# A squared-ReLU MLP on one core: the norm's factor moves from the up-projection to the sums of the down-projection, the ReLU to ScalarE, the residual to DRAM

## The chip, the core and the metric

The kernel runs on one core of a Trainium2 chip. Five engines with queues of their own work side by side: TensorE (PE, with its weight loads as PEld), VectorE (DVE), ScalarE (ACT), GpSimd (POOL) and SyncE (SP), which here only issues transfers. Each engine takes its instructions strictly in the order of its queue: one that waits holds back all behind it. The metric is the device time of one execution in microseconds (us).

## The reference

One layer of a hybrid decoder trunk, 1024 tokens of 1024 channels in fp32: a combined input projection feeds a pooling mixer and a gated linear recurrence, whose outputs go through an output projection onto the residual h; then come the squared-ReLU MLP, which the change touches, a per-layer gate and a final norm.

```
h = h + concat([y_pool, y_lru]) @ w_out
z = h * rsqrt(mean(h*h) + eps) * norm_mlp_g
h = h + square(relu(z @ w_up)) @ w_down          # 1024 -> 4096 -> 1024
z = rms_norm(h, norm_ple_g)
h = h + sigmoid(z @ w_ple_gate + b_ple_gate) * (p @ w_ple_proj)
out = rms_norm(h, norm_final_g)
```

The factor r = rsqrt(mean(h*h) + eps) is one positive number per token. So square(relu(r*u)) = r*r*square(relu(u)), and a token's r*r can be taken out of the sum over the 4096 channels of the down-projection.

## The kernel before, in words

**Layout.** Activations are kept transposed: channels on the 128 partitions, tokens along the free axis. `H[0..7]` is the residual, eight tiles of 128 x 1024; FIRST and SECOND are its two halves of 512 tokens. Every operand of a large product is split into a high and a low part, `hi` by ACT (line 185) and `lo = x - hi` by DVE (line 186), and a product takes three matmuls (hi by hi, hi by lo, lo by hi). On PE each matmul of 128x128 by 128x512 follows the last after 0.216 us.

**Stages by time.** Input projection, recurrence and pooling to 141 us; output projection with the residual add and the squares for the MLP's norm to about 224 us; up-projection to 512.33 us; down-projection to 802.5 us; the gate's products (`ps_e`, `ps_j`) to 900 us; then the last output.

**Up-projection** (`up_first`, `up_pair`, `up_double`, `up_last`). The 4096 channels are 16 pairs of tiles (`NPAIR`). A pair is a 2x2 block product by a fast scheme with seven products P1 to P7; pairs 4, 6, ... 14 go through `up_double`, which shares work with the pair before; the odd ones after them open with line 1003. A pair's result is `cc`, 128 x 2048 (quadrants c11, c12, c21, c22). `finish_up` then does `max(cc, 0) * R` on DVE over all 2048 columns (line 861, R the norm's factor), squares on ACT (line 863), some sums and differences on DVE that are the operands of the down-projection, and stores to DRAM (`act`). `copy` (line 880) and line 1003 move a PSUM result to its place on ACT; line 1003 makes the start value in bank `ps_b_u`, on which P6 of that pair accumulates.

**Norm** (`Norm.rstd`). The token sums come from a small matmul (`n_ps`, in the first half of the gate's norm `n2_ps`, in its second half `n2b_ps`); ACT takes the square root (line 482), DVE the reciprocal, and R is made by a transpose.

**Down-projection** (`down(n)`, 14 kinds: chunk c = 0 and 1, in each P1, P2, P4, P6, P7, P5, P3, each for four q). One product is 24 matmuls, 5.18 us. Before, every product is added straight into the residual `H` on DVE (line 843). In the last two kinds, P5 and P3 of chunk 1, finished tiles are squared at once for the next norm (`ple_in`, lines 440 and 443), while ACT and DVE also split the weights `wd_P_q` of the coming products and the first weights `wg_0`, `wg_1` and `proj` of the gate.

**Order.** The program is written in Python under a tile scheduler that orders each engine's queue when the program is built, by dependence and the place in the text; no order is written out by hand except for `pin`, `issue_after` and the like.

Of the kernel before, what the change touches and what calls it, by code (L numbers as in the profile page):

```python
# [63 lines left out]
def block_kernel(  # L64
# [44 lines left out]
    def pairs(tiles):  # L109
# [15 lines left out]
        ]  # L125
        for c in range(NCHUNK)
    ]
    edge = ctx.enter_context(tc.tile_pool(name="edge", bufs=1, side="right"))
    spread = edge.tile([P, 72], F32, name="edge")
    B = pairs(space("y", 12, F32R)) + pairs(space("y2", 4, F32R, "right"))  # L130
# [93 lines left out]
    def twice(x):  # L224
        return x.unsqueeze(1).broadcast_to([P, 2, x.shape[-1]])
# [203 lines left out]
    class Norm:  # L429
# [42 lines left out]
            in_order.clear()  # L472
            return [(hs, o)]

        def rstd(self, out, parts):


            for hs, o in parts:
                few = self.few(hs)
                nc.vector.tensor_copy(few, o[:, :16])  # L480
                nc.vector.tensor_tensor(few, few, o[:, 16:], ALU.add)
                nc.scalar.activation(few, few, AF.Sqrt, bias=eps, scale=1.0 / D)
                nc.vector.reciprocal(few, few)
                nc.vector.transpose(out[:, hs], few.unsqueeze(2).broadcast_to([P, 16, 32]))

# [372 lines left out]
    def finish_up(m, cc):  # L858

        c, t = divmod(m, CHUNK // 2)  # L860
        nc.vector.scalar_tensor_tensor(cc, cc, 0.0, twice(R), ALU.max, ALU.mult)
        for x in (cc[:, 1], cc[:, 0]):
            nc.scalar.activation(x, x, AF.Square)
        x11, x12, x22 = cc[:, 0, FIRST], cc[:, 0, SECOND], cc[:, 1, SECOND]
        t2 = E[1][:, FIRST]
        t4_t1 = E[0].rearrange("p (y s) -> p y s", y=2)
        x2 = cc[:, 1].rearrange("p (y s) -> p y s", y=2)
        dv(ALU.subtract, x12, x22, x12)
        dv(ALU.add, t2, x12, x11)
        dv(ALU.subtract, t4_t1, x2, twice(t2))  # L870

        def store_up():
            for g, x in enumerate((cc[:, 0].rearrange("p (y s) -> p y s", y=2), x2, t4_t1)):
                nc.sync.dma_start(ACT[c][g][t // 2][:, t % 2], x)
            nc.sync.dma_start(ACT[c][3][t // 2][:, t % 2, 0], t2)

        return store_up

    def copy(to, ps):
        nc.scalar.activation(by(to, ps), got(ps), AF.Copy)  # L880

    leave("y2")
    e1, *up_spare[:] = space("wu", 3, F32, "right")
# [133 lines left out]
    def up_double(m):  # L1017

        before = up_sums(m - 1)[3]
        cc, c11, c12, c21, c22 = up_sums(m)  # L1020
        left, right = QUARTERS
        a = bank(f"ps_a_u{m}")
        up_product(m, "P1", a)
        b = banks(f"ps_b_u{m}")[:, :HALF]
        nc.scalar.activation(b, a, AF.Copy, scale=-1.0)
        w12 = weights()
        z = bank(f"ps_z_u{m}")
        sub_product(z[:, left], w12[0], 1)
        v = banks(f"ps_v_u{m}")[:, left]
        nc.scalar.activation(v, z[:, left], AF.Copy, scale=-1.0)  # L1030
        d = bank(f"ps_d_u{m}")
        up_product(m, "P5", d)
        copy(c22, d)
        w54 = weights()
        sub_product(z[:, left], w12[1], 2, True)
        sub_product(z[:, right], w54[0], 5)
        nc.scalar.activation(by(c21[:, right], z[:, right]), got(z[:, right]), AF.Copy, scale=-1.0)
        up_product(m, "P6", b, more=True)
        copy(c12, b)
        x = bank(f"ps_x_u{m}")[:, left]  # L1040
        sub_product(x, w54[1], 4)
        copy(c21[:, left], x)
        w63 = weights()
        sub_product(v, w63[0], 6, True)
        take(before[:, right], v, before[:, right], True)
        sub_product(z[:, right], w63[1], 3, True)
        both = before.rearrange("p (b a j) -> p b a j", b=2, a=2)
        add(both, z.rearrange("p (b j a) -> p b a j", b=2, a=2))
        store = finish_up(m - 1, up_sums(m - 1)[0])
        up_product(m, "P2", a, more=True)  # L1050
        copy(c11, a)
        store()
        sub_product(v, weights()[0], 7, True)
        both = c21.rearrange("p (b a j) -> p b a j", b=2, a=2)
        add(both, got(v).unsqueeze(1).broadcast_to([P, 2, 2, P]))
        if m == NPAIR - 2:
            restore(up_sums(m + 1)[3])
        up_product(m, "P3", d, more=True)
        take(c12, d, c12)
        up_product(m, "P7", b, more=True)  # L1060
        take(c22, b, c22)
        add_got(c21, b)

    def up_pair(m):
        if m - 1 in DOUBLES:
            return up_double(m)
        cc, c11, c12, c21, c22 = up_sums(m)
        a, d = up_open(m)
        b = chains[m]
        if m > DOUBLES[0]:  # L1070
            finish_up(m - 1, up_sums(m - 1)[0])()
        elif m > 1:
            up_fourth(m - 1)()
        else:
            norm.rstd(R, [x for hs in HALVES for x in norm.sums(hs)])
            leave("hl")
            extra.extend(space("x", 2, F32R))
        up_product(m, "P6", b, more=True)
        copy(c12, b)
        up_product(m, "P2", a, more=True)  # L1080
        copy(c11, a)
        for n in ((), (3,), (1, 2), (4,))[m] if m < 4 else ():
            double_operand(n)
        up_product(m, "P3", d, more=True)
        take(c12, d, c12)
        if m == 1:
            finish_up(0, up_sums(0)[0])()
        up_product(m, "P7", b, more=True)
        take(c22, b, c22)
        if m in DOUBLES:  # L1090
            copy(c21, chains.pop(m))
# [83 lines left out]
    def down(n):  # L1175
# [6 lines left out]
        for q in range(NQ):  # L1182
            w = weights() if n or q else asked.pop(0)
            behind = (upper[0], lowest[0]) if n < 5 and n + q else ()
            if last and kind == "P5":
                if q == 0:
                    for k in range(2):
# [19 lines left out]
                        load_w(0, ij, 1 + q)  # L1207
            if kind == "P1":
                copy(u, x)
                add_got(c11, x)  # L1210
            elif kind == "P2":
                add_got(c11, x)
            elif kind == "P6":
                add_got(u, x)
                add(c12, u)
            elif kind == "P7":
                add_got(u, x)
                add(H[2 * q + 1].rearrange("p (y s) -> p y s", y=2), twice(u))
            elif kind == "P4":
                add_got(c21, x)  # L1220
            elif kind == "P5":
                add_both(h_all[:, 2 * q : 2 * q + 2, SECOND], x)
            else:
                add_got(c12, x)
            for tp in (FIRST_AHEAD[n] if n < 2 else AHEAD)[q]:
                prepare(n + 1, tp, behind)
            if last:
                for o in IN.get((kind, q), ()):
                    ple_in(o, FIRST, norm2)
                if (kind, q) == ("P3", 2):  # L1230
                    norm2.gather(FIRST, T[1][:, FIRST], True)

    Z, ple, late, quad = [], [], [], []

# [22 lines left out]
    up_first()  # L1257
    for m in range(1, NPAIR - 1):
        up_pair(m)
    up_last()  # L1260
    norm2 = Norm("n2", T[0], T[1:2])
    for n in range(NOPS):
# [400 lines left out]
```

## Time and profile before

| | us |
|---|---|
| median of 3 runs (914.81 to 915.29) | 915.27 |
| the profiled execution: its time | 915.34 |
| its span | 913.6 |
| PE busy in the span | 905.2 (99%) |
| DVE busy | 738.8 (81%) |
| ACT busy | 477.9 (52%) |
| POOL busy | 39.6 (4%) |
| mean granted TensorE clock | 0.999 |

The span runs from the first to the last profiled instruction; 915.34 - 913.6 = 1.74 us lie around it. A busy share says little by itself: an engine that is busy 81% may have its idle time where nobody needs it, or may be late at one place for which PE waits. What counts is the chain that ended last and the waits of the engine on it.

### The profile page before, as it was taken

How to read it: one execution, taken by the hardware profiler on the slowest of the kernel's cores; microseconds unless marked ns; L12 is line 12 of the kernel's file. 1: busy time of each engine (PE TensorE's matmuls, PEld its weight loads, DVE VectorE, ACT ScalarE, POOL GpSimd, SP SyncE). 2: the span in 40 equal slices, each digit the busy share in tenths (PEclk: the TensorE clock that was granted, in tenths of full speed). 3: DMA queues.
4: the chain of work that ended last, by engine and by line, in shares of the span. 5: the costliest groups of instructions: out<-in, count | busy, mean ns of one | idle time of the engine just before them, and what ended most of it. 6: DMA issues, size and time to landing. Idle time of an engine off the chain costs nothing.

```text
span 913.6 us, 11556 instructions
## 1 busy us (share of the span) xinstructions
PE 905.2 (99%) x4329; PEld 791.3 (87%) x4329; DVE 738.8 (81%) x949; ACT 477.9 (52%) x631; POOL 39.6 (4%) x62
## 2 busy tenths in 40 slices
PE   9999999999999999999999999999999999999996
PEld 7888888888888988988988888888888888888886
DVE  7999974668997769678688989899876579799676
ACT  6569892447564555555445644354343436655223
POOL 4400001000000000000000000000000000000001
PEclk9999999999999999999999999999999999999999
DMA  8311145214368778777684987466633341031353
GB/s 272 104 47 33 60 150 150 81 46 109 109 177 253 192 187 235 165 224 204 185 245 164 362 326 277 138 201 198 200 118 114 116 161 47 1 124 62 96 172 136
DMA packets 56872, 142.49 MB, mean 156 GB/s; under 512 B 4976, under 2 KB 9968, under 8 KB 56816
## 3 DMA queue, kind: packets, MB, share of 16 engines
q1 hardware_dynamic: 52848, 132.05, 44.8%
q0 software_dynamic: 2736, 8.91, 5.4%
q10 hardware_dynamic: 1232, 0.79, 0.4%
q8 instruction: 34, 0.56, 0.2%
q14 instruction: 22, 0.18, 0.1%
HBM read 106.08 MB, written 35.65 MB: 155 GB/s over the span
## 4 chain that ended last, share of the span: by engine, by line
PE 95%; DVE 3%; issue 1%; DMA 1%; SPq 0%; ACT 0%; POOLq 0%; POOL 0%; DVEq 0%
PE ps_P_d L399 32%; PE ps_i L399 9%; PE ps_b_u L399 9%; PE ps_d_u L399 9%; PE ps_a_u L399 9%; PE ps_o L399 8%; PE ps_e L399 8%; PE ps_l L399 3%; PE ps_z_u L940 2%; PE ps_e L1398 2%; PE ps_P_u L399 2%; PE ps_v_u L940 1%; PE ps_j L399 1%; DVE y L189 1%; PE ps_g L662 1%
## 5 line engine op out<-in xcount | busy, mean ns | idle before, releaser
L399 PE MATMUL ps_P_d<-a,wd_P_hi 128*128 128x512 f32 x880 | 261.7, 379 | 0.0
L399 PEld LDWEIGHTS ps_P_d<-a,wd_P_hi 128*128 128x128 f32 x880 | 166.3, 189 | 23.6
L399 PE MATMUL ps_P_d<-a,wd_P_lo 128*128 128x512 f32 x440 | 166.8, 379 | 0.0
L399 PEld LDWEIGHTS ps_P_d<-a,wd_P_lo 128*128 128x128 f32 x440 | 83.2, 189 | 11.8
L399 PE MATMUL ps_a_u<-y,wu_P 128*128 128x512 f32 x360 | 82.6, 379 | 0.0
L399 PE MATMUL ps_b_u<-a,wu_P 128*128 128x512 f32 x360 | 82.4, 379 | 0.0
L399 PEld LDWEIGHTS ps_a_u<-y,wu_P 128*128 128x128 f32 x360 | 67.6, 189 | 9.3
L399 PEld LDWEIGHTS ps_b_u<-a,wu_P 128*128 128x128 f32 x360 | 67.5, 189 | 9.3
L843 DVE TENSOR_TENSOR t_h<-t_h,ps_P_d 128x512 f32<-128x512 f32 (+1 forms) x56 | 42.7, 762 | 37.5 <-PE ps_P_d L399 37.5
L186 DVE TENSOR_TENSOR a<-wd,a 128x1024 fp32r<-128x1024 f32 x56 | 67.2, 1222 | 0.9 <-ACT a L185 0.6
L399 PE MATMUL ps_i<-a,wi_hi 128*128 128x512 f32 x256 | 66.1, 381 | 0.0
L399 PE MATMUL ps_o<-y,wo_hi 128*128 128x512 f32 x256 | 65.7, 379 | 0.0
L186 DVE TENSOR_TENSOR wu_P<-wu_raw,wu_P 128x512 fp32r<-128x512 f32 x45 | 30.8, 687 | 39.4 <-ACT wu_P L185 39.4
L185 ACT ACTIVATE a<-wd 128x1024 fp32r<-128x1024 f32 x56 | 57.9, 1049 | 7.0 <-PE ps_P_d L399 7.0
L185 ACT ACTIVATE wd_P_hi<-wd 128x1024 fp32r<-128x1024 f32 x24 | 25.3, 1056 | 58.6 <-PE ps_P_d L399 58.6
L399 PEld LDWEIGHTS ps_i<-a,wi_hi 128*128 128x128 f32 x256 | 48.1, 189 | 8.0 <-PE ps_g L662 0.3
L399 PEld LDWEIGHTS ps_o<-y,wo_hi 128*128 128x128 f32 x256 | 48.4, 189 | 6.8
L399 PE MATMUL ps_d_u<-a,wu_P 128*128 128x512 f32 x180 | 41.3, 379 | 0.0
L399 PE MATMUL ps_d_u<-y,wu_P 128*128 128x512 f32 x180 | 41.3, 379 | 0.0
L185 ACT ACTIVATE wu_P<-wu 128x512 fp32r<-128x512 f32 x48 | 29.3, 624 | 22.3 <-DVE wu L218 11.7
L399 PE MATMUL ps_i<-a,wi_lo 128*128 128x512 f32 x128 | 38.1, 379 | 0.0
L399 PE MATMUL ps_o<-y,wo_lo 128*128 128x512 f32 x128 | 38.1, 379 | 0.0
(285 smaller groups left out, 1655.5 us busy)
## 6 DMA issues: line engine op xcount, KB each, us to landing
wd<-act SPq DMA_DIRECT2D x56, 512.0 KB, 5.5
act<-t_h SPq DMA_DIRECT2D x48, 512.0 KB, 5.9
wu<-in_w_up SPq DMA_DIRECT2D x16, 512.0 KB, 5.0
wd<-in_w_down SPq DMA_DIRECT2D x16, 512.0 KB, 6.8
wu_raw<-in_w_up SPq DMA_DIRECT2D x15, 512.0 KB, 4.8
t_h<-in_xT SPq DMA_DIRECT2D x14, 512.0 KB, 4.9
wg_raw<-in_w_gate SPq DMA_DIRECT2D x10, 512.0 KB, 3.3
wi_raw<-in_w_in SPq DMA_DIRECT2D x9, 512.0 KB, 3.3
```

Of the source, the lines that this page charges most:

```text
L185: first = pin(nc.scalar.activation(hi, src, AF.Copy))
L186: lowest[:] = [pin((eng or nc.vector).tensor_tensor(lo, src, f32(hi), ALU.subtract)).ins]
L189: lowest[:] = [pin(nc.vector.scalar_tensor_tensor(lo, src, g, f32(hi), ALU.mult, ALU.subtract)).ins]
L399: ins = nc.tensor.matmul(ps, w, turns(z[:, hs]), start=first and z is zhi and w is whi, stop=last and w is wlo, skip_group_check=more,)
L662: nc.tensor.matmul(x, w[r, o * P : (o + 1) * P], turns(z[r, at : at + HALF]), start=n == 0, stop=n == 2)
L843: (eng or nc.vector).tensor_tensor(to, to if y is None else y, x, ALU.add)
L940: nc.tensor.matmul(ps, kblk(w, t), turns(z[:, t]), start=t == x == 0 and not more, stop=t == 1 and x == 2, skip_group_check=more,)
L1398: nc.tensor.matmul(pg, z, turns(quad[x == 1][:, k]), start=n == 0, stop=n == 3 * NT - 1, skip_group_check=True)
```

## The change

- `finish_up` no longer multiplies by R. DVE's pass over 2048 columns (line 861) goes; ACT does Relu over 1536 columns (c12, c21, c22; for the first pair over all 2048) and one Square over 2048. The Relu of c11 rides on its copy from PSUM. The last pair does `max(x, 0) * x` in one DVE instruction and nothing on ACT.
- The norm's factor is squared: for the MLP's norm, `1 / (mean + eps)`, with a DVE multiply and add in place of ACT's Sqrt and its table load.
- The residual is stored to DRAM: eight stores of 512 KB on SP's queue (`held_h`), which the scheduler places between the last loads of `wo_raw` and the loads of the up-projection's `wu_raw`, each before one of these loads.
- In chunk 0 of the down-projection the products that were added to H are first written to it, by ACT copies (c11, c21, c12, c22), so H holds sums without the residual.
- In chunk 1, `settle` multiplies each finished half tile by R on DVE (16 instructions of 512 columns) and brings the residual back: 14 half tiles by an accumulating transfer of 256 KB on POOL's queue (`grow`, from `held_h`), and the SECOND halves of tiles 4 and 6 by two transfers on SP's queue into a spare buffer and a DVE add. The squares for the gate's norm and the split of the gate's operand then wait for these transfers.

```diff
--- before.py
+++ after.py
@@ -125,6 +125,7 @@
         ]
         for c in range(NCHUNK)
     ]
+    held_h = [dram.tile([P, S], F32, name=f"held{o}") for o in range(NT)]
     edge = ctx.enter_context(tc.tile_pool(name="edge", bufs=1, side="right"))
     spread = edge.tile([P, 72], F32, name="edge")
     B = pairs(space("y", 12, F32R)) + pairs(space("y2", 4, F32R, "right"))
@@ -472,14 +473,17 @@
             in_order.clear()
             return [(hs, o)]
 
-        def rstd(self, out, parts):
+        def rstd(self, out, parts, square=False):
 
 
             for hs, o in parts:
                 few = self.few(hs)
                 nc.vector.tensor_copy(few, o[:, :16])
                 nc.vector.tensor_tensor(few, few, o[:, 16:], ALU.add)
-                nc.scalar.activation(few, few, AF.Sqrt, bias=eps, scale=1.0 / D)
+                if square:
+                    nc.vector.tensor_scalar(few, few, 1.0 / D, EPS, ALU.mult, ALU.add)
+                else:
+                    nc.scalar.activation(few, few, AF.Sqrt, bias=eps, scale=1.0 / D)
                 nc.vector.reciprocal(few, few)
                 nc.vector.transpose(out[:, hs], few.unsqueeze(2).broadcast_to([P, 16, 32]))
 
@@ -858,9 +862,13 @@
     def finish_up(m, cc):
 
         c, t = divmod(m, CHUNK // 2)
-        nc.vector.scalar_tensor_tensor(cc, cc, 0.0, twice(R), ALU.max, ALU.mult)
-        for x in (cc[:, 1], cc[:, 0]):
-            nc.scalar.activation(x, x, AF.Square)
+        if m == NPAIR - 1:
+            nc.vector.scalar_tensor_tensor(cc, cc, 0.0, cc, ALU.max, ALU.mult)
+        else:
+            whole = cc.rearrange("p c s -> p (c s)")
+            rest = whole if m == 0 else whole[:, HALF:]
+            nc.scalar.activation(rest, rest, AF.Relu)
+            nc.scalar.activation(whole, whole, AF.Square)
         x11, x12, x22 = cc[:, 0, FIRST], cc[:, 0, SECOND], cc[:, 1, SECOND]
         t2 = E[1][:, FIRST]
         t4_t1 = E[0].rearrange("p (y s) -> p y s", y=2)
@@ -876,8 +884,8 @@
 
         return store_up
 
-    def copy(to, ps):
-        nc.scalar.activation(by(to, ps), got(ps), AF.Copy)
+    def copy(to, ps, fn=AF.Copy):
+        nc.scalar.activation(by(to, ps), got(ps), fn)
 
     leave("y2")
     e1, *up_spare[:] = space("wu", 3, F32, "right")
@@ -1048,7 +1056,7 @@
         add(both, z.rearrange("p (b j a) -> p b a j", b=2, a=2))
         store = finish_up(m - 1, up_sums(m - 1)[0])
         up_product(m, "P2", a, more=True)
-        copy(c11, a)
+        copy(c11, a, AF.Relu)
         store()
         sub_product(v, weights()[0], 7, True)
         both = c21.rearrange("p (b a j) -> p b a j", b=2, a=2)
@@ -1072,13 +1080,13 @@
         elif m > 1:
             up_fourth(m - 1)()
         else:
-            norm.rstd(R, [x for hs in HALVES for x in norm.sums(hs)])
+            norm.rstd(R, [x for hs in HALVES for x in norm.sums(hs)], square=True)
             leave("hl")
             extra.extend(space("x", 2, F32R))
         up_product(m, "P6", b, more=True)
         copy(c12, b)
         up_product(m, "P2", a, more=True)
-        copy(c11, a)
+        copy(c11, a, AF.Relu)
         for n in ((), (3,), (1, 2), (4,))[m] if m < 4 else ():
             double_operand(n)
         up_product(m, "P3", d, more=True)
@@ -1182,6 +1190,9 @@
         for q in range(NQ):
             w = weights() if n or q else asked.pop(0)
             behind = (upper[0], lowest[0]) if n < 5 and n + q else ()
+            if last and kind == "P3" and q == 0:
+                for x in (2, 3):
+                    nc.sync.dma_start(behind_h[x], held_h[2 * x][:, SECOND])
             if last and kind == "P5":
                 if q == 0:
                     for k in range(2):
@@ -1207,21 +1218,44 @@
                         load_w(0, ij, 1 + q)
             if kind == "P1":
                 copy(u, x)
-                add_got(c11, x)
+                if c == 0:
+                    copy(c11, x)
+                else:
+                    add_got(c11, x)
             elif kind == "P2":
                 add_got(c11, x)
+                if last:
+                    settle(2 * q, FIRST)
             elif kind == "P6":
                 add_got(u, x)
-                add(c12, u)
+                if c == 0:
+                    nc.scalar.activation(c12, u, AF.Copy)
+                else:
+                    add(c12, u)
             elif kind == "P7":
                 add_got(u, x)
-                add(H[2 * q + 1].rearrange("p (y s) -> p y s", y=2), twice(u))
+                if c == 0:
+                    add(c21, u)
+                    nc.scalar.activation(c22, u, AF.Copy)
+                else:
+                    add(H[2 * q + 1].rearrange("p (y s) -> p y s", y=2), twice(u))
+                if last:
+                    settle(2 * q + 1, FIRST)
             elif kind == "P4":
-                add_got(c21, x)
+                if c == 0:
+                    copy(c21, x)
+                else:
+                    add_got(c21, x)
             elif kind == "P5":
                 add_both(h_all[:, 2 * q : 2 * q + 2, SECOND], x)
+                if last:
+                    settle(2 * q + 1, SECOND)
+                    if q > 1:
+                        behind_h[q] = up_spare[0][:, HALVES[q - 2]]
             else:
                 add_got(c12, x)
+                if last:
+                    settle(2 * q, SECOND, behind_h.get(q))
             for tp in (FIRST_AHEAD[n] if n < 2 else AHEAD)[q]:
                 prepare(n + 1, tp, behind)
             if last:
@@ -1229,6 +1263,17 @@
                     ple_in(o, FIRST, norm2)
                 if (kind, q) == ("P3", 2):
                     norm2.gather(FIRST, T[1][:, FIRST], True)
+
+    behind_h = {}
+
+    def settle(o, hs, old=None):
+
+        x = H[o][:, hs]
+        dv(ALU.mult, x, x, R[:, hs])
+        if old is None:
+            grow(x, held_h[o][:, hs])
+        else:
+            dv(ALU.add, x, x, old)
 
     Z, ple, late, quad = [], [], [], []
 
@@ -1257,6 +1302,8 @@
     up_first()
     for m in range(1, NPAIR - 1):
         up_pair(m)
+        if 2 < m <= NT + 2:
+            nc.sync.dma_start(held_h[m - 3], H[m - 3])
     up_last()
     norm2 = Norm("n2", T[0], T[1:2])
     for n in range(NOPS):
```

PE keeps its 2656 rows. Three places show what the scheduler made of it. `a<-b` is what an instruction writes and reads.

**ACT between pair 4 and pair 5, before** (and so between 6 and 7, ... 14 and 15). `ps_a_u`, `ps_b_u`, `ps_d_u` are PSUM results, `wu_P` the split weights, `t_h` the pair's tiles:

```order
217 L880 ACTIVATE t_h<-ps_a_u_2357 128x512
218 L185 ACTIVATE wu_P_2509<-wu_1767 128x512
219 L185 ACTIVATE wu_P_2525<-wu_1768 128x512
220 L863 ACTIVATE t_h<-t_h 128x1024 x2
221 L185 ACTIVATE wu_P_2545<-wu_1768 128x512
222 L185 ACTIVATE wu_P_2563<-wu_1767 128x512
223 L1003 ACTIVATE ps_b_u_2561<-ps_a_u_2543 128x512
224 L185 ACTIVATE wu_P_2589<-wu_1768 128x512
225 L880 ACTIVATE t_h<-ps_d_u_2544 128x512
226 L185 ACTIVATE wu_P_2605<-wu_1768 128x512
227 L863 ACTIVATE t_h<-t_h 128x1024 x2
```

The same place in the change (line 870 is the Relu, 871 the Square, 888 and 1011 are the old 880 and 1003):

```order
218 L870 ACTIVATE t_h<-t_h 128x1536
219 L871 ACTIVATE t_h<-t_h 128x2048
220 L888 ACTIVATE t_h<-ps_a_u_2363 128x512
221 L186 ACTIVATE wu_P_2514<-wu_1775 128x512
222 L186 ACTIVATE wu_P_2530<-wu_1776 128x512
223 L186 ACTIVATE wu_P_2569<-wu_1775 128x512
224 L186 ACTIVATE wu_P_2551<-wu_1776 128x512
225 L870 ACTIVATE t_h<-t_h 128x1536
226 L1011 ACTIVATE ps_b_u_2567<-ps_a_u_2549 128x512
227 L871 ACTIVATE t_h<-t_h 128x2048
228 L888 ACTIVATE t_h<-ps_d_u_2550 128x512
```

A Relu, which waits for DVE's last add into pair 4, now stands ahead of the copy into `ps_b_u`, and a Square of 2048 columns directly behind it.

**ACT at the end of the down-projection, before** (`wd_P_2_hi`, `wd_P_3_hi` belong to the last two products, 440 and 443 are squares for the gate's norm):

```order
514 L185 ACTIVATE wd_P_2_hi<-wd_4146 128x1024
515 L440 ACTIVATE t_h<-t_h 128x512
516 L185 ACTIVATE wd_P_3_hi<-wd_4147 128x1024
517 L443 ACTIVATE t_h<-t_h 128x512
518 L185 ACTIVATE proj_6222<-t_h 128x1024
519 L185 ACTIVATE proj_6224<-t_h 128x1024
520 L185 ACTIVATE proj_6226<-t_h 128x1024
521 L185 ACTIVATE proj_6228<-t_h 128x1024
522 L185 ACTIVATE wg_0_hi<-wg_0_raw 128x1024
523 L443 ACTIVATE t_h<-t_h 128x512
```

The same place in the change:

```order
540 L186 ACTIVATE wd_P_2_hi<-wd_4147 128x1024
541 L444 ACTIVATE t_h<-t_h 128x512
542 L441 ACTIVATE t_h<-t_h 128x512
543 L186 ACTIVATE wd_P_3_hi<-wd_4148 128x1024
544 L444 ACTIVATE t_h<-t_h 128x512
545 L186 ACTIVATE wg_0_hi<-wg_0_raw 128x1024
546 L186 ACTIVATE wg_1_hi<-wg_1_raw 128x1024
547 L186 ACTIVATE proj_6259<-t_h 128x1024
548 L186 ACTIVATE proj_6261<-t_h 128x1024
```

The four `proj` splits now stand behind `wg_0` and `wg_1`, and the squares in rows 542 and 544 wait for the accumulating transfers of the SECOND halves of H[0] and H[2].

**PE in the gate's products, before** (the token sums of the gate's norm for the second half, `n2b_ps`):

```order
2387 L399 MATMUL ps_e_2_6356<-ple_5999,wg_2_hi 128x512
2388 L399 MATMUL ps_e_2_6356<-ple_6000,wg_2_hi 128x512
2389 L399 MATMUL ps_e_2_6356<-ple_5999,wg_2_lo 128x512
2390 L471 MATMUL n2b_ps_6408<-sums_5989,same 128x32
2391 L399 MATMUL ps_e_3_6415<-proj_6222,proj_6226 128x512
2392 L399 MATMUL ps_e_3_6415<-proj_6223,proj_6226 128x512
```

In the change:

```order
2416 L400 MATMUL ps_e_3_6452<-ple_6022,wg_3_lo 128x512
2417 L400 MATMUL ps_e_3_6452<-ple_6022,wg_3_hi 128x512
2418 L472 MATMUL n2b_ps_6445<-sums_6012,same 128x32
2419 L400 MATMUL ps_e_3_6452<-ple_6023,wg_3_hi 128x512
2420 L400 MATMUL ps_e_3_6452<-ple_6022,wg_3_lo 128x512
```

The small matmul stands 28 rows later: behind the six `proj` matmuls and 22 of the 24 gate matmuls of `ps_e_3`. On DVE the four `lo` splits of `proj` now stand behind the last add into H, ahead of the sums that this matmul reads.

## The prediction

> **What bounds the kernel now.** I read the page's head, then the chain of waits, then PE's own waits.
>
> ```profile
> PE 905.2 (99%) x4329; PEld 791.3 (87%) x4329; DVE 738.8 (81%) x949; ACT 477.9 (52%) x631; POOL 39.6 (4%) x62
> PE 95%; DVE 3%; issue 1%; DMA 1%; SPq 0%; ACT 0%; POOLq 0%; POOL 0%; DVEq 0%
> PE ps_l L538 <- PEq L1649: 0.8, 1, 0.8
> PE ps_l L593 <- ACT a L529: 0.3, 1, 0.3
> 234.83 0.61 DVE wu_P L186
> 235.44 0.04 issue
> 235.49 4.58 PE ps_P_u L399 x20
> 512.33 290.18 PE ps_P_d L399 x1344
> ```
>
> PE is on 95% of the chain; its two waits that the trace lists, 1.1 us, lie in the recurrence, far ahead of the change. The whole down-projection is one piece, 290.18 us over 1344 matmuls, 0.216 us each, without a hole. From the output projection on DVE ends a wait once, at 234.83: `lo` of the first up weights, and the starts of PE's matmuls leave some 0.4 us there and 0.1 us at the start of the down-projection. The change leaves PE its rows, so what it frees on DVE can give back **0.5 us at most**. The question is which waits it makes.
>
> **What is removed and added, by engine.**
>
> ```profile
> L861 DVE SCALAR_TENSOR_TENSOR t_h<-t_h,rstd 128x2048 f32<-128x2048 f32 x16 | 36.6, 2287 | 0.6 <-ACT t_h L880 0.6
> L863 ACT ACTIVATE t_h<-t_h 128x1024 f32<-128x1024 f32 x32 | 32.1, 1051 | 7.0 <-DVE t_h L861 6.9
> L443 ACT ACTIVATE t_h<-t_h 128x512 f32<-128x512 f32 x21 | 13.2, 626 | 14.4 <-DVE t_h L1317 7.3 <-DVE t_h L444 7.0
> L482 ACT ACT_TABLE_LOAD x3 | 3.8, 1283 | 0.1
> ```
>
> DVE: less 15 passes of 2.29 us (the last pair keeps one), less twelve of chunk 0's adds, more 16 multiplies of 512 columns and two adds. ACT: 512 columns take 0.63 and 1024 take 1.05, so 0.83 us per 1000 columns and 0.2 fixed; a Relu of 1536 is estimated at 1.48, a Square of 2048 at 1.91. A pair needs 3.4 us of ACT in place of 2.1, and 3.4 in all where it needed 2.29 + 2.1 on two engines: the pair's result is ready earlier, not later. No such Relu is in the trace; its bounds are 1.05 and 2.1 (one and two of 1024). [...]
>
> **Square of the factor, stores: nothing.** The DVE multiply and add replaces a table load of 1.28 us in the same queue. A store's issue on SP is short:
>
> ```profile
> 159.84 1.22 DVE L804 TENSOR_TENSOR t_h<-t_h,ps_o 128x1024 f32<-128x1024 f32 x1 [10.10 <-PE ps_o L399]
> 160.98 1.22 DVE L186 TENSOR_TENSOR wo_lo<-wo_raw,wo_hi 128x1024 fp32r<-128x1024 f32 x1
> 162.23 23.49 SPq L204 DMA_DIRECT2D wo_raw<-in_w_out  x4
> 218.42 0.80 SPq L254 DMA_DIRECT2D t_h<-in_w_up  x2
> 224.21 0.63 ACT L185 ACTIVATE wu_P<-t_h 128x512 fp32r<-128x512 f32 x1 [0.67 <-ACT y L188]
> ```
>
> Each store waits for an add into H; behind it in SP's queue stands a load that waits for a DVE split that comes after that add (160.98 behind 159.84), so the store is never what the load waits for; it adds 0.4 us of issue. The tightest is the store ahead of 218.42: those two loads can come 0.4 later by its issue and 1 by sharing the transfer engines, and ACT reads their tile at 224.21, 5.8 us after their issue. 0, with 0.5 as the upper bound.
>
> **The seam from pair 4 to pair 5**, six times.
>
> ```profile
> 414.86 0.69 DVE L843 TENSOR_TENSOR t_h<-t_h,ps_z_u 128x512 f32<-128x512 f32 x1
> 416.06 2.29 DVE L861 SCALAR_TENSOR_TENSOR t_h<-t_h,rstd 128x2048 f32<-128x2048 f32 x1
> 418.86 1.29 DVE L186 TENSOR_TENSOR wu_P<-wu,wu_P 128x512 fp32r<-128x512 f32 x2
> 424.93 0.68 DVE L843 TENSOR_TENSOR t_h<-t_h,ps_b_u 128x512 f32<-128x512 f32 x1
> 425.28 0.58 ACT L1003 ACTIVATE ps_b_u<-ps_a_u 128x512 f32<-128x512 f32 x1 [1.90 <-PE ps_a_u L399]
> 427.67 2.75 PE L399 MATMUL ps_b_u<-a,wu_P 128*128 128x512 f32 x12
> 501.80 1.46 PE L399 MATMUL ps_d_u<-y,wu_P 128*128 128x512 f32 x6
> ```
>
> The copy ended at 425.86 and PE took the bank at 427.67: 1.8 us of slack. Now it stands behind the Relu, which waits for the add of 424.93. I replayed the two queues with the durations above (two of 512 on DVE take 1.29, so the next starts after 0.60; two of 1024, below, 2.35, so after 1.14): Relu(3) from 415.6, Square(3) to 418.9, DVE starts on its result at 418.95 and runs nine instructions, eight of 512 and one of 1024, of which that add is the last, to 425.0; Relu(4) to 426.5, the copy to 427.05. That leaves 0.6 us: no stall. Where the add is up to 0.3 later, it still holds. In the last pair the same order brings the copy some 0.1 behind PE's start at 501.80, and DVE's sums for the first down product come as late as before: **0.15 us** for both.
>
> **Chunk 0** trades DVE adds for ACT copies of 0.6 us, in a stage whose products take 5.18 us: 0.
>
> **The end of the down-projection.** Here transfers enter ACT's queue.
>
> ```profile
> 787.00 0.69 DVE L843 TENSOR_TENSOR t_h<-t_h,ps_P_d 128x512 f32<-128x512 f32 x1 [0.24 <-PE ps_P_d L399]
> 792.03 1.06 ACT L185 ACTIVATE wd_P_hi<-wd 128x1024 fp32r<-128x1024 f32 x1 [3.66 <-PE ps_P_d L399]
> 792.19 0.69 DVE L843 TENSOR_TENSOR t_h<-t_h,ps_P_d 128x512 f32<-128x512 f32 x1 [3.08 <-PE ps_P_d L399]
> 802.33 1.06 ACT L185 ACTIVATE wg_hi<-wg_raw 128x1024 fp32r<-128x1024 f32 x1 [2.58 <-PE ps_P_d L399]
> 802.51 5.18 PE ps_e L399 x24
> rstd<-in_w_up POOLq DMA_DIRECT2D x3, 256.0 KB, 4.8
> wu_raw<-in_w_up POOLq DMA_DIRECT2D x7, 512.0 KB, 7.7
> wu_raw<-in_w_up POOLq DMA_DIRECT2D x1, 256.0 KB, 4.2
> L228 POOL DMA_DIRECT2D rstd<-in_w_up x3 | 2.8, 1033 | 123.0 <-DMA rstd<-in_w_up 123.0
> 788.00:800.00 12.00, 12.00 (x58) 10.50 (x57) 7.54 (x8) 7.32 (x9) 0.00 (x0) 1.00 0.00 1
> ```
>
> The third product of P3 starts at 792.1 and the last at 797.3. H[0]'s SECOND half: add at 787.0, multiply at 787.6 to 788.3, transfer 4.2 to 4.8 (the rows of 256 KB on POOL's queue, which accumulate too; DMA is idle from 788 on, 1 GB/s) and up to 1.0 for POOL's own instruction: landed at 792.5 to 794.1. Its square then lets `wd_P_3_hi` go at 793.2 to 794.6, not at 792.03; hi is needed at 797.3, lo at 797.75: over 1 us left. H[2]: add 792.2, landed 797.7 to 799.3, square, `wg_0_hi` to 800.8 at the latest, `lo` to 802.0; PE needs it at 802.9. Margin 0.9 to 2.3: no stall, and each us beyond counts in full. [...]
>
> **The sums of the gate's second half**: the one term that I expect to see.
>
> ```profile
> 796.62 2.35 DVE L186 TENSOR_TENSOR proj<-t_h,proj 128x1024 fp32r<-128x1024 f32 x2
> ...
> 803.71 0.68 DVE L843 TENSOR_TENSOR t_h<-t_h,ps_P_d 128x512 f32<-128x512 f32 x1
> 815.10 0.17 DVE L461 TENSOR_TENSOR sums<-edge,sums 128x16 fp32r<-128x16 f32 x1
> 822.04 0.02 PE n2b_ps L471
> 822.07 6.57 PE ps_e L399 x30
> 855.66 0.59 PE L399 MATMUL ps_e<-a,wg_hi 128*128 128x512 f32 x2
> ```
>
> Before, the sums were ready at 815.28 and PE came for them at 822.04: 6.8 us early. In the change PE comes 28 matmuls later, at 822.04 + 28 x 0.216 = 828.1. DVE's last add into H follows `wg_0`'s lo, H[4]'s residual and the first half's sums, so it starts at 802.8 to 804.2 (before 803.71). Between it and the end of the sums its queue now holds 38 instructions, that add among them: 20 of 512 columns at 0.60 (12.0), nine of 1024 at 1.14 (10.3; the four `proj` splits among them, of which two ran at 796.62 before), two transposes and a reduction (1.9) and six short ones at 0.17 (1.0): 25.2, up to 0.3 more where one reads its predecessor's result. Ready at 828.0 to 829.7, and 0.2 more for the weight load that reads them. PE waits 0.1 to 1.8 us; I take **1.1**, from above the middle, since every wait that the replay missed adds. What follows (the factor, eight multiplies, the splits) shifts by the 7 us too, but ends near 852, ahead of the first use at 855.7.
>
> **The sum.** 915.34 + 0.15 + 1.1 = 916.6 for an execution like the profiled one, whose time is 0.07 above the median of the runs shown: 916.5. The terms at zero have upper bounds of 0.5 (loads), 1.8 (seam, if each of six is 0.3 late) and 1 (a transfer), and the gain at most 0.5.
>
> **Rivals.** A measurement of this kernel tells 0.2%, 1.83 us, from no change.
>
> *Slower at the gate's sums, more than I take.* Same place; decides from 1.7 us of stall on, which takes sums ready after 829.6. For it: the replay leaves out every wait between ACT and DVE over 25 us, and a second transfer 1 us late moves the add. Against: the replay has no gap left on DVE, and its intervals are those of full queues. 915.3 + 0.15 + 2.5 = 918.0. Chance 0.20.
>
> *Slower in the seams.* Relu takes 2.1 and the add ends 0.4 later: then the copy is late by 0.4 each time, 2.4 us in six, on top of the 1.1: 918.9. It decides once Relu and add are 0.6 later together. Against: DVE loses 2.29 us per pair there. Chance 0.10.
>
> *Slower by late transfers.* The accumulating transfer takes 7 us, near the 7.7 of POOL's 512 KB row: the lo of `wg_0` is 2 late and the sums with it: 918.5. The DMA share of 0.00 is against it. Chance 0.08.
>
> *Faster.* No wait arises, and 0.5 is given back at 235 and 516: 914.8. That is no measurable gain either; beyond 0.2% I see no source but PE's own idle time, 0.03.
>
> *No effect at all*, every wait covered: 915.3, inside the forecast's range.
>
> **How the numbers follow.** The likeliest, no measurable change by a wait of 0 to 1.7 us, has 0.59 with the covered cases; its own range is 914.9 to 917.1. The three slower ones have 0.38, faster 0.03. The range 914.9 to 918.7 takes in the first and the third rival whole.
>
> **What would show it.** Right: the chain of waits has a piece of DVE (`sums`, L462) directly ahead of `n2b_ps`, about 1 us, at 828 to 830, and PE's pieces unbroken from 242 to 828. The Relu of 1536 at 1.4 to 1.5 us and the copy of line 1011 ending ahead of PE's P6. Transfers on POOL's queue landing within 5 us. Wrong: waits of PE on ACT `ps_b_u` in the up-projection, on DVE `wg_lo` at 803, on `wd_P_lo` at 797; or a hole ahead of 512 because the stores to DRAM delay a weight load.

## The result

| | before | the change |
|---|---|---|
| median of 11 runs, us | 915.34 (914.81 to 915.52) | 918.12 (916.71 to 920.82) |
| the profiled execution: its time, us | 915.34 | 916.71 |
| its span, us | 913.6 | 914.9 |
| PE / DVE / ACT busy, us | 905.2 / 738.8 / 477.9 | 905.4 / 709.8 / 502.0 |

The change is **slower**: the ratio is 1.0038 with a 95% interval of 1.0026 to 1.0049. It lies inside the predicted range (914.9 to 918.7), but "no measurable change" was wrong. Five of the 11 executions lie above that range. Two things are to be explained: the profiled execution, which happens to be the fastest, is 1.4 us slower than the profiled one before, and the executions now spread over 4.1 us (six from 916.7 to 918.1, five from 919.8 to 920.8), where the kernel before has 0.7. In what follows two executions far above all others, 1612 us of one variant and 3341 us of the kernel before, are left out.

The page's head, the chain's engines and PE's waits of the profiled execution of the change (engine, line, what it waited for: us in all, how often, the longest):

```profile
PE 905.4 (99%) x4329; PEld 791.4 (87%) x4329; DVE 709.8 (78%) x942; ACT 502.0 (55%) x643; POOL 51.8 (6%) x76
PE 90%; DVE 5%; issue 2%; ACT 2%; DMA 1%; POOLq 0%; POOL 0%; DVEq 0%; ACTq 0%
PE n2b_ps L472 <- DVE sums L462: 0.9, 1, 0.9
PE ps_l L542 <- PEq L1696: 0.8, 1, 0.8
PE ps_a_u L400 <- DVE wu_P L187: 0.6, 1, 0.6
```

DVE is busy 29 us less and PE just as long (905.4 against 905.2). PE's share of the chain falls from 95% to 90%, although PE is as busy as before: for stretches its work hangs on DVE and ACT. Two waits are new: 0.9 us at the small matmul of the gate's second half, and 0.6 us on the split of a weight in the up-projection. Together 1.5 us, against 1.37 by which this execution is slower than the profiled one before.

The groups of the new instructions (busy us, mean ns of one, idle before):

```profile
L871 ACT ACTIVATE t_h<-t_h 128x2048 f32<-128x2048 f32 x15 | 28.6, 1905 | 0.3
L870 ACT ACTIVATE t_h<-t_h 128x1536 f32<-128x1536 f32 x14 | 20.8, 1486 | 4.4 <-DVE t_h L847 4.4
```

The seams between pairs in ACT's timeline (start, length in us; the copy is that of line 1011):

```profile
424.80 1.49 ACT L870 ACTIVATE t_h<-t_h 128x1536 f32<-128x1536 f32 x1
426.20 0.58 ACT L1011 ACTIVATE ps_b_u<-ps_a_u 128x512 f32<-128x512 f32 x1
```

The chain in order of time, with PE behind that copy, and a transfer of the residual with what follows it:

```profile
427.41 2.59 PE ps_b_u L400 x12
...
794.28 3.70 DMA t_h<-held
798.61 1.05 ACT wg_hi L186
```

The Relu took 1.49 us and the Square 1.91; the copy into `ps_b_u` ended at 426.78, 0.63 ahead of PE. The residual of H[2] landed at 798.0. These three came as forecast. The next place did not.

### The profile page after: what moved, and what is told of

It is laid out like the page before. It is cut to its first block, busy times and chain, and to the rows that moved or that the text cites. A ratio compares the mean times of both kernels' runs of the same rounds, so it can differ in the third digit from the quotient of the medians.

```text
span 914.9 us, 11579 instructions
## 1 busy us (share of the span) xinstructions
PE 905.4 (99%) x4329; PEld 791.4 (87%) x4329; DVE 709.8 (78%) x942; ACT 502.0 (55%) x643; POOL 51.8 (6%) x76
## 4 chain that ended last, share of the span: by engine, by line
PE 90%; DVE 5%; issue 2%; ACT 2%; DMA 1%; POOLq 0%; POOL 0%; DVEq 0%; ACTq 0%
PE ps_P_d L400 31%; PE ps_i L400 9%; PE ps_b_u L400 8%; PE ps_o L400 8%; PE ps_d_u L400 8%; PE ps_a_u L400 8%; PE ps_e L400 5%; PE ps_l L400 3%; PE ps_e L1445 2%; PE ps_z_u L948 2%; PE ps_P_u L400 2%; PE ps_l L597 1%; PE ps_v_u L948 1%; PE ps_g L666 1%; ACT y L189 1%
## 5 line engine op out<-in xcount | busy, mean ns | idle before, releaser
L847 DVE TENSOR_TENSOR t_h<-t_h,ps_P_d 128x512 f32<-128x512 f32 (+1 forms) x48 | 37.2, 774 | 32.4 <-PE ps_P_d L400 32.4
```

The source lines that it names most:

```text
L847: (eng or nc.vector).tensor_tensor(to, to if y is None else y, x, ALU.add)
```

## The experiments

All kernels were compared with runs of the kernel before on the same chip (medians 915.4 to 915.6). To see where time goes, the start of each matmul on PE is compared with that of the same matmul in the profile of the kernel before; a step in this difference is time lost at that place.

### The change once more: where the spread comes from

No edit.

> The change itself once more, for the profile of an execution and the spread: its 11 runs lie in two groups, 916.7 to 918.1 and 919.8 to 920.8 us, where the kernel before has 914.8 to 915.5, and the mean granted TensorE clock of the upper group is lower (0.996 to 0.997 against 0.997 to 0.999). Theory A: every execution has PE's two waits of 0.58 us (at 499) and 0.92 us (at 829), 1.4 us in all, and in some the clock is taken down for a few us behind a wait, which adds about 3; an execution of the upper group then shows a stretch with a granted clock under 1.00 and the same two waits. Theory B: the upper group is a late transfer; such an execution shows a wait of 2 to 4 us more at 797 to 829 and a clock of 1.00 in every stretch.

Measured: 917.99 to 920.13 us, and the profiled execution was the one of 920.13. PE's waits in it:

```profile
PE n2b_ps L472 <- DVE sums L462: 1.8, 1, 1.8
PE ps_a_u L400 <- DVE wu_P L187: 0.6, 1, 0.6
```

A table of it by stretch (us; the sum and the busy us of PE, PEld, DVE, ACT and POOL with counts; granted clock, DMA share, GB/s):

```profile
828.00:830.00 2.00, 1.24 (x6) 0.75 (x4) 1.97 (x4) 1.06 (x2) 0.00 (x0) 1.00 0.48 190
830.00:832.00 2.00, 0.94 (x5) 0.86 (x6) 2.00 (x5) 1.35 (x2) 0.00 (x0) 1.00 0.00 0
832.00:834.00 2.00, 2.00 (x7) 1.59 (x6) 1.50 (x5) 0.48 (x1) 0.00 (x0) 0.54 0.42 119
834.00:836.00 2.00, 2.00 (x8) 1.57 (x7) 1.49 (x3) 1.97 (x4) 0.00 (x0) 0.61 0.37 143
836.00:838.00 2.00, 2.00 (x11) 1.76 (x10) 1.97 (x4) 1.36 (x2) 0.00 (x0) 1.00 0.00 0
```

Both theories held in part. The wait at the small matmul is longer, 1.8 us. And 1.1 us after it ends the granted clock falls to 0.50 and stays there for 3.4 us: PE is "busy" all the time, but does 7 and 8 matmuls in 2 us instead of 11. In stretches of 0.25 us the two in which the clock changes are these, so it fell at about 832.16 and rose at about 835.58:

```profile
832.00:832.25 0.25, 0.25 (x3) 0.22 (x2) 0.25 (x2) 0.00 (x0) 0.00 (x0) 0.83 0.00 0
835.50:835.75 0.25, 0.25 (x2) 0.22 (x1) 0.19 (x1) 0.24 (x2) 0.00 (x0) 0.84 0.00 0
```

Counted at the starts of the matmuls:

| lost at | the change, 916.71 | once more, 920.13 |
|---|---|---|
| up to 236 (start, recurrence) | -0.4 | +0.4 |
| 499, the weight's split | 0.7 | 0.7 |
| the gate's sums | 1.2 | 2.1 |
| clock at 0.50 | 0 | 1.7 |
| in all | 1.5 | 4.9 |

The first row varies without any edit: it is -0.3 to 0.7 in the ten traces of the other runs below. Part of it is the clock again. At the start of each trace the matmuls follow each other after 0.43 us, and after 0.22 only from a moment that differs from one execution to the next (by the trace's record of the granted clock): 3.7 us from the start of the span in the kernel before, 4.1 in the change, 6.1 in the change once more. The four traces in which it comes after 6.1 us (5 matmuls between 4 and 6 us, where the others have 6 to 9) have 0.4 to 0.7 in this row, the others -0.4 to 0.3.

Why the wait is 0.9 in one execution and 1.8 in the other shows in ACT's timeline, here of the change, of the same kernel once more, and of the kernel `pair14` below, where the wait was 2.6:

```profile
816.85 1.06 ACT L186 ACTIVATE wg_hi<-wg_raw 128x1024 fp32r<-128x1024 f32 x1 [0.32 <-DMA wg_raw<-in_w_gate]
817.81 0.61 ACT L444 ACTIVATE t_h<-t_h 128x512 f32<-128x512 f32 x1
```

```profile
818.57 1.06 ACT L186 ACTIVATE wg_hi<-wg_raw 128x1024 fp32r<-128x1024 f32 x1 [1.32 <-DMA wg_raw<-in_w_gate]
819.53 0.61 ACT L444 ACTIVATE t_h<-t_h 128x512 f32<-128x512 f32 x1
```

```profile
819.58 1.06 ACT L186 ACTIVATE wg_hi<-wg_raw 128x1024 fp32r<-128x1024 f32 x1 [1.92 <-DMA wg_raw<-in_w_gate]
820.55 0.62 ACT L444 ACTIVATE t_h<-t_h 128x512 f32<-128x512 f32 x1
```

ACT's queue has the split of `wg_3` ahead of squares for the gate's sums (line 444), and that split waits for its load: idle 0.32, 1.32 and 1.92 us, the square behind it starts 0.96, 0.96 and 0.97 us after it, and PE's wait is 0.92, 1.82 and 2.56. The load is issued when DVE's split of `wg_2` has freed its buffer (812.10 to 813.32 in the change; issue at 813.35), and that DVE split stands behind the four `proj` splits (DVE's timeline of the change, and behind it the issue on SP's queue):

```profile
807.46 4.63 DVE L187 TENSOR_TENSOR proj<-t_h,proj 128x1024 fp32r<-128x1024 f32 x4 [1.12 <-ACT proj L186]
812.10 1.22 DVE L187 TENSOR_TENSOR wg_lo<-wg_raw,wg_hi 128x1024 fp32r<-128x1024 f32 x1
```

```profile
813.35 0.33 SPq L205 DMA_DIRECT2D wg_raw<-in_w_gate  x1
```

The load landed 3.4, 4.4 and 5.0 us after its issue. The profile of the change is the exception: in the eight other traces with this order (the change once more and seven of the kernels below) ACT is idle there for 1.3 to 1.9 us, so a wait near 0.9 is rare among the traces and one of about 2 common. With `pair13` (idle 1.58, wait 2.1) and the two kernels below in which PE comes 8 matmuls, 1.7 us, later (idle 1.62 and 1.48, waits 0.5 and 0.4) the waits still follow the idle time. But no run changed the load alone, and why it lands sooner in one execution is not shown.

### A wait and nothing else, in the kernel before

```diff
             keep(ins)
+            if self.name == "n2b":
+                way = [dram.tile([P, 32], F32R, name=f"way{x}") for x in range(2)]
+                for to, at in ((way[0], both), (way[1], way[0]), (both, way[1])):
+                    nc.gpsimd.dma_start(to, at)
             return ins.ins
```

> The kernel before with one thing added: the sums that the small matmul of the gate's second half reads are sent over three small transfers (16 KB, POOL's queue) before PE may read them. They were ready 6.8 us before PE came; three transfers of about 3 us each make PE wait some 2 to 3 us there, and nothing else of the change is in it. If a wait costs its own length: 915.4 plus the wait. If a wait of 1.8 us or more also takes the clock down: granted clock 0.5 for 3.4 us from about 1 us behind the wait, 1.7 us more, and a time of 915.4 + wait + 1.7, about 919.5 for a wait of 2.5.

Measured: 917.67, 917.76, 919.96 and 920.14 us. PE's queue is that of the kernel before; the profiled execution (920.14) shows the wait:

```profile
PE n2b_ps L475 <- DMA sums<-way: 2.4, 1, 2.4
```

and the same table the clock:

```profile
822.00:824.00 2.00, 0.45 (x3) 0.05 (x1) 1.29 (x2) 0.58 (x2) 0.56 (x1) 1.00 0.63 242
824.00:826.00 2.00, 1.13 (x5) 1.02 (x6) 0.80 (x3) 1.85 (x3) 0.00 (x0) 0.90 0.11 8
826.00:828.00 2.00, 2.00 (x7) 1.55 (x6) 1.93 (x5) 1.09 (x2) 0.00 (x0) 0.50 0.00 0
828.00:830.00 2.00, 2.00 (x9) 1.69 (x8) 2.00 (x3) 1.11 (x2) 0.00 (x0) 0.75 0.00 0
```

Steps: 0.4 at the start, 2.5 for the wait, 1.8 for the clock. By their times two executions cost the wait alone (915.4 + 2.4 = 917.8) and two the wait and the clock; the mean granted clock of the whole execution, 0.998 in the first two and 0.996 in the others, agrees. So the upper group needs none of the change's Relu, stores or transfers of the residual: here it came with a wait of PE alone, in two of four executions by their times.

With one hop more:

```diff
-                way = [dram.tile([P, 32], F32R, name=f"way{x}") for x in range(2)]
-                for to, at in ((way[0], both), (way[1], way[0]), (both, way[1])):
+                way = [dram.tile([P, 32], F32R, name=f"way{x}") for x in range(3)]
+                for to, at in ((way[0], both), (way[1], way[0]), (way[2], way[1]), (both, way[2])):
```

> The kernel before with the sums sent over four transfers instead of three, so that PE waits some 6 us (2.4 and one hop of 3.4 to 3.7 more). With a wait of 2.4 two of four executions lay at 917.7 (the wait alone) and two at 920.1 (granted clock 0.50 for 3.4 us behind it). [...] If the drop is a matter of chance at any wait: two groups again, one at 921.5.

Measured: 919.43, 919.70, 920.27 and 920.43 us. In the profiled execution (920.43) the wait was 3.2 us, not 6:

```profile
PE n2b_ps L475 <- DMA sums<-way: 3.2, 1, 3.2
```

The second hop between DRAM tiles took 2.1 us, and the small matmul stands six matmuls, 1.3 us, later on PE than in the run with three transfers, so the numbers expected do not apply. The steps are 3.3 for the wait and 1.8 for the clock, which fell 0.1 us after PE went on. The wait alone would be about 918.6, and all four times are above it; but the waits of the other three are not known, and their mean clocks (0.997 to 0.998) do not decide whether each had the drop.

### The matmul that waits, put later

```diff
-LATER = ((), (), (0, 1), (2, 3), (4, 5), (6, 7), ())
+LATER = ((), (), (), (0, 1, 2, 3), (4, 5), (6, 7), ())
...
                 ple_proj(hs, o, pj)
+                if g == 0 and n == 4:
+                    norm2.rstd(R, norm2.sums(SECOND))
                 ple_gate(g, hs, o, pg)
...
-                    norm2.rstd(R, norm2.sums(SECOND, T[2][:, SECOND]))
+                    norm2.gather(SECOND, T[2][:, SECOND])
```

> The small matmul of the gate's second half is put 8 rows later on PE, behind the six proj matmuls (829.8 instead of 828.1). If the wait there is what the sums cost, it goes: the fastest runs come down by 0.9 us to 915.8. Theory A with the wait at 829 as what takes the clock down: the upper group goes too, median near 916. Theory A with the wait at 499 as the cause, or theory B: the upper group stays near 919.

Measured: 916.34 us median (915.83 to 916.85), ratio 1.0010, 1.0001 to 1.0020. A wait of 0.5 us is left in its trace, none with a clock under 1.00 behind it, and no execution above 917. The same, inside `ps_e_4` after three of its eight blocks (16 rows later than in the change):

> The change with the small matmul 16 rows later on PE (inside ps_e_4, at about 831.5), where it was 8 rows later in the run that left a wait of 0.5 us. The sums come at 829.2 to 831.7 in the traces so far, so a wait is left in the slowest executions alone. If the wait and the clock behind it are the whole difference: 915.9 to 916.3, no execution above 916.8, only the 0.6 us at 499 left. If the later factor now makes the second half's operands late: PE waits at 856 and above for splits, 917 and more.

Measured: **915.96 us** (915.60 to 916.38), ratio 1.0006, 0.9997 to 1.0015. PE's waits in the trace:

```profile
PE ps_l L542 <- PEq L1700: 0.8, 1, 0.8
PE ps_a_u L400 <- DVE wu_P L187: 0.6, 1, 0.6
PE ps_l L597 <- ACT a L533: 0.2, 1, 0.2
```

Nothing waits at the gate any more, and moving one small matmul, with the factor that comes from it, takes back 2.2 of the 2.8 us. No wait of PE in this trace shows that the factor comes later.

### Why the sums are late: the residual in the spare buffer

```diff
-            if last and kind == "P3" and q == 0:
-                for x in (2, 3):
-                    nc.sync.dma_start(behind_h[x], held_h[2 * x][:, SECOND])
...
-                    if q > 1:
-                        behind_h[q] = up_spare[0][:, HALVES[q - 2]]
```

with the matmul later as in the kernel with 8 rows.

> The change with all 16 halves of the residual brought back by the accumulating transfers, so that no half waits in the spare buffer of the pool that the four proj splits reuse, and the small matmul 8 rows later. If the spare buffer is what puts the proj splits behind the last add, the splits run at 794 to 802 again, the sums are ready some 4 us earlier, and no wait is left there in any execution: 915.8 to 916.1, all runs within 0.8. If the last two transfers come late instead: a wait at 829 of 1 us or more.

Measured: 916.83 us (916.23 to 917.87). DVE's timeline in this kernel:

```profile
798.44 2.36 DVE L187 TENSOR_TENSOR proj<-t_h,proj 128x1024 fp32r<-128x1024 f32 x2 [1.12 <-ACT proj L186]
803.69 1.18 DVE L187 TENSOR_TENSOR proj<-t_h,proj 128x1024 fp32r<-128x1024 f32 x1
805.38 1.22 DVE L187 TENSOR_TENSOR proj<-t_h,proj 128x1024 fp32r<-128x1024 f32 x1
825.59 0.17 DVE L462 TENSOR_TENSOR sums<-edge,sums 128x16 fp32r<-128x16 f32 x1
```

Two `proj` splits are early again and all four are done by 806.6 (812.1 in the change); the sums come at 825.6 instead of 829.1, and there is no wait at the small matmul. From the last add into H to the sums DVE now has 31 instructions instead of 38. So the cause named is right: the two halves of the residual that wait in the spare buffer keep the pool open whose memory `proj` takes, and the splits fall behind the last add into H. (In the profile of the change ACT stands idle for 2.66 us ahead of its first `proj` split, until DVE has added the spare buffer at 806.3.) The edit moved other work of ACT and DVE too, so the 3.5 us are not those of the four splits alone. It is no better as a kernel, 0.9 us above the one with the matmul 16 rows later; its profiled execution lost 0.3 us at 808, where PE takes the first half's small matmul. The rest I did not trace.

### The wait in the up-projection

```diff
-        if m == NPAIR - 1:
+        if m >= NPAIR - 2:
             nc.vector.scalar_tensor_tensor(cc, cc, 0.0, cc, ALU.max, ALU.mult)
```

> Only pair 14 goes back to one DVE instruction max(x, 0) * x in place of ScalarE's Relu and Square, so that DVE need not wait for the Square at 490. The wait of 0.58 us at 499 goes: the fastest runs 916.1. Theory A with the wait at 499 as what takes the clock down: no upper group; with the wait at 829, or theory B: the upper group stays near 919.5.

Measured: 918.66 us (917.82 to 921.13); the wait of 0.6 us was still there. The profiled execution had a wait of 2.6 us at the gate and the clock at 0.50 for 3.4 us behind it. The edit missed: what DVE waits for is pair 13's Square, since a pair is finished during the next one. Together with the matmul 8 rows later:

> Both edits together. If the two waits are the whole steady cost, the fastest runs are at 915.2 to 915.4, like the kernel before. Theory A: the spread shrinks to that of the kernel before (0.7 us) and the verdict is the same to 0.05%. Theory B, or a cost that lies elsewhere (the stores, the transfers): runs of 918 and above remain.

Measured: 916.85 us (916.30 to 917.49), 1.0016. The wait of 0.6 at 499 and one of 0.4 at the gate are left; the spread is 1.2 us.

Pair 13 on DVE (`if m in (NPAIR - 3, NPAIR - 1)`):

> The change with pair 13 (finished during pair 14, at 486) back on DVE in one instruction, so that DVE need not wait 0.8 us for ScalarE's Square at 490. The edit of pair 14 came too late in the program to touch this wait: it was still 0.6 us. If DVE's wait for the Square is what makes the weight's split late: the wait of 0.6 us at 499 goes, and all executions come down by 0.6. If DVE's order at that seam is the cause: it stays. The wait at 829 and the clock behind it are not touched: 917.3 to 920.

Measured: 923.01 us (921.69 to 923.99). The wait at 499 became 0.4, and four new ones stand at the start of the down-projection:

```profile
PE n2b_ps L472 <- DVE sums L462: 2.1, 1, 2.1
PE ps_P_d L400 <- DVE a L187: 2.0, 4, 0.8
PE ps_l L542 <- PEq L1696: 0.8, 1, 0.8
PE ps_a_u L400 <- DVE wu_P L187: 0.4, 1, 0.4
```

The scheduler orders the queues anew when a duration changes, and the first operands of the down-projection came late. It tells nothing clean of the wait at 499. With half of the pair's work on each engine the other queues keep their order (with the matmul 16 rows later):

```diff
+        elif m == NPAIR - 3:
+            x, y = cc[:, 0], cc[:, 1]
+            nc.scalar.activation(x[:, HALF:], x[:, HALF:], AF.Relu)
+            nc.scalar.activation(x, x, AF.Square)
+            nc.vector.scalar_tensor_tensor(y, y, 0.0, y, ALU.max, ALU.mult)
```

> The run with the small matmul 16 rows later (915.96 us, the wait of 0.6 us at 499 left), and pair 13 split between two engines: ScalarE does Relu (512 columns) and Square (1024) of c11 and c12, VectorE max(x, 0) * x of the other 1024 columns, in its idle time at 487 to 489. The queue orders everywhere else stay as they were. ScalarE is done 1.7 us earlier (488.4 instead of 490.1). If DVE's wait for the Square is what makes the split at 499 late: no wait of PE from 236 to the end, 915.3 to 915.5, the same as the kernel before within 0.05%. If a later add or the pair's order sets it: 0.3 to 0.6 us remain, 915.9.

Measured: 915.75 us (915.39 to 918.08), 1.0007, 0.9998 to 1.0016. The wait at 499 is gone and another has come (PE's waits, ACT's timeline, PE's timeline):

```profile
PE ps_d_u L400 <- ACT t_h L893: 0.5, 1, 0.5
```

```profile
498.39 1.49 ACT L875 ACTIVATE t_h<-t_h 128x1536 f32<-128x1536 f32 x1
499.91 1.91 ACT L876 ACTIVATE t_h<-t_h 128x2048 f32<-128x2048 f32 x1
501.73 0.58 ACT L893 ACTIVATE t_h<-ps_d_u 128x512 f32<-128x512 f32 x1
```

```profile
502.36 2.86 PE L400 MATMUL ps_d_u<-y,wu_P 128*128 128x512 f32 x12 [0.52 <-ACT t_h L893]
```

DVE's wait for the Square was the cause at 499. Two of the 11 executions, 917.46 and 918.08, lie well above the other nine (to 916.52); neither was profiled, and what they lost is not known. Now Relu and Square of pair 14 start 1 us earlier and stand together ahead of the copy that empties `ps_d_u`, where they stood on either side of it. With pair 14 on DVE as well:

> The split of pair 13 removed the wait at 499 but left one of 0.52 us at 501.8, where PE waits for ScalarE's copy of ps_d_u behind Relu and Square of pair 14. Here pair 14 is also done on DVE in one instruction, in DVE's idle time from 500.2 to 501.85. If those two pairs are the whole cost of the up-projection: no listed wait of PE behind the recurrence, 915.2 to 915.4, 0.5 us under the run with pair 13 alone, and no difference from the kernel before. If DVE's 2.3 us make the first operands of the down-projection late: waits on DVE `a` at 512 to 520 and 916 or more.

Measured: 918.75 us (916.92 to 918.86). No wait is left in the up-projection; 3.5 us are lost from 512 to 516.3, at the first operands of the down-projection (in the waits: `ps_P_d` on DVE `a`, 1.9 us in three, and on ACT `a`, 0.3). No version of the change that I ran beats the kernel before; the nearest are the same as it within their intervals.

## Why the prediction was wrong

- **What bounds.** Right: PE's queue without a hole, at most 0.5 us to win. DVE's 29 us less work won nothing.
- **Durations, seams, stores, transfers.** Right. Relu 1.49 and Square 1.91 us against 1.48 and 1.91; the copy 0.63 ahead of PE against 0.6; the transfer of H[2] landed at 798.0, within 797.7 to 799.3. The eight stores cost PE nothing: the differences at the starts show no step from 160 to 236. The rival of late transfers falls, and so does that of the seams: no wait on `ps_b_u`.
- **The last pair, 0.15 us.** The place was right to a pair, the instruction and the size wrong: 0.7 us, at a weight's split 2 us ahead of the copy that I looked at. I had replayed the queues of ACT and DVE for pairs 4 and 5 and carried the result over; at the last pairs DVE also has `restore` to do (line 914, three sums in DVE's queue from 493.8 on). The wait for the Square (0.8 us of idle DVE at 490) is as long at 418, between pairs 4 and 5, where PE loses nothing; that `restore` takes the reserve is read from the queue, no run leaves it out. The copy I had named turned into the bound (0.5 us) as soon as the split was out of the way.
- **The sums of the gate's second half, 1.1 us.** This is the step that failed. The place, the cause on DVE (four `proj` splits behind the last add), the 38 instructions and the wait of the fastest execution (0.92) were right; the last add began at 803.19, within 802.8 to 804.2. But the replay took DVE's queue alone, held ACT to be ready and so had no gap on DVE: 25.2 to 25.5 us from the last add to the sums. The profile of the change has 26.1, with 1.1 of it idle, for ACT's first `proj` split; the eight other traces with these 38 instructions have 27.1 to 27.7, with 1.9 to 2.5 idle. There ACT has the split of `wg_3` ahead of the squares, and its load, issued only when the same late DVE has freed a buffer, takes 4.4 to 5.0 us. So the term is 0.9 to 2.6 us in the traces, mostly about 2, not 0.1 to 1.8. My first rival had this place and 2.5 us, at a chance of 0.20; its argument ("the replay leaves out every wait between ACT and DVE") was the right one, and the weight too small. That its 918.0 lies beside the median is partly luck, since it holds the 0.15 of the last pair, which was 0.7.
- **What no case had**: the granted clock. I priced a wait at its own length. In the five traces with a wait of 1.8 us or more at the small matmul the clock was 0.50 for 3.4 us behind it, which cost 1.7 us more, about the gap between the two groups of executions.
- An execution of the change is in its parts 0.7 + 0.9 to 2.6 + 0 or 1.7, on a start that varies by some 0.5 either way. The median one (918.12) was not profiled; as an estimate, 915.34 + 0.7 + about 2 = 918.0 takes it in without the drop of the clock, which is then the upper group's alone.

## What to carry to other kernels

When a chain is moved close to the engine that bounds, replay every queue on it, and count a load in front of such a queue with its slowest landing, not its median. A buffer that is kept a little longer can move work of another stage: look for what else takes its memory. If a small, early-placed instruction on the bounding engine waits, put it later before anything else is done: here 16 rows brought back 2.2 of 2.8 us.

## What the runs showed of the hardware

**A wait of PE can cost more than its length.** Behind the wait of 0.9 us at the small matmul the clock stayed at 1.00; behind those of 1.8, 2.1, 2.4, 2.6 and 3.2 us it was 0.50 for 3.4 us, 1.7 us of time. It fell 0.1 to 1.5 us after PE went on (us from the span's start; the times of the clock from its mean in stretches of 0.25 us for `pair14` and the change once more, of 2 us for the others):

| trace | wait of PE, us | PE goes on | clock falls to 0.50 | rises to 1.00 |
|---|---|---|---|---|
| the change | 0.9 | 829.3 | no | |
| the change once more | 1.8 | 831.1 | 832.16 | 835.58 |
| pair 13 on DVE (`pair13`) | 2.1 | 834.3 | 835.8 | 839.2 |
| the kernel before, three transfers | 2.4 | 824.9 | 825.6 | 829.0 |
| pair 14 on DVE (`pair14`) | 2.6 | 832.1 | 832.79 | 836.2 |
| the kernel before, four transfers | 3.2 | 826.5 | 826.6 | 830.0 |

Between 10 and 900 us no other stretch of 2 us in the 13 traces has a clock under 1.00. That holds for `split1314` too, where PE waits four times, 2.2 us in all and at most 0.9 at once, from 512 to 520 us. Between 0.9 and 1.8 us no trace shows a wait of PE. Nor did the clock fall behind every longer one: in the kernel before with three transfers two of four executions (917.67 and 917.76 us, mean clock 0.998) cost by their times the wait alone. That fits the two groups of the change; but no execution of this kind was profiled, and what decides whether the clock falls is not shown.

**Accumulating transfers beside a busy DVE.** The 14 transfers of 256 KB from POOL's queue landed in 4.1 us (median), as quick as such rows in the trace before (4.2 and 4.8). The seven beside which DVE was busy for 98 to 100% of the time took 3.8 to 4.5 us; the chain's one took 3.7, with DVE busy for 41%.
